# A delta rule's instructions put in order per engine by a list scheduler inside the kernel, with one projection ahead of them and one behind

## The chip, the core and the metric

The kernel runs on one core of a Trainium2 chip. The metric is the time of one execution on the device in microseconds, as the median of three runs. Engines: PE (tensor engine, its weight loads shown apart as PEld), DVE (vector), ACT (scalar), POOL (GpSimd), SP (issues the weight transfers).

## The reference

Two blocks run one after the other in fp32. The first has two layers over 256 context and 256 latent tokens; its even layer mixes a windowed attention with a delta rule ("rwkv7"). The stage in question is this recurrence, run forward and backward, first over the context, then over the latent tokens, for 8 heads of 64:

```
def rwkv7_scan(f, d, s0, reverse):
    def step(state, inp):
        r_t, w_t, k_t, v_t, kk_t, a_t = inp
        sa = jnp.einsum('bhvk,bhk->bhv', state, -kk_t)
        state = (state * w_t[:, :, None, :] + sa[..., None] * (kk_t * a_t)[:, :, None, :]
                 + v_t[..., None] * k_t[:, :, None, :])
        return state, jnp.einsum('bhvk,bhk->bhv', state, r_t)
    ...
    s_last, ys = lax.scan(step, s0, xs, reverse=reverse)
```

Its inputs come from a shifted projection of the tokens, its output is normalised per head, gated, joined with the attention's and multiplied by `w_out`. The feed-forward parts, the odd layer and the second block follow; the change leaves them alone.

## The kernel before

The scan is written as blocks of 64 tokens. There are sixteen passes n, in the order of three loops (L1062 to L1066): tile t (two heads) from 0 to 3, sequence s (context, latent), direction d. A pass is two functions.

`rwkv_par` (L819) needs no state. Preparation: the decays (`pw` L832, `sg`, a scan `cs`, three exponentials), the rates (`pa` L850, `ic`), the scaled vectors `kr` and `bk`, their products `gp` (L883) with masked copies into `GK` and `Gt`, and transposes (`pbk`, `pkv`). Inverse: a product `px`, then five doubling levels (L931 to L944), each a DVE transposition `Tp`, eight matmuls `pq`, a masked DVE copy `Qm` and eight matmuls `psx`; then `pwu`, `pqm` and `QM`. `rwkv_rec` (L973) takes the state through four blocks: matmul `yp` (L986), a copy by DVE and one by ACT (L993), the next matmul; then it copies to `yN`.

Passes overlap as far as buffers allow. PSUM banks go by rings (L180): the preparation takes banks 0, 1, 2 in turn, the inverse of pass n bank 3 + n % 3, the recurrence bank 6, everything else of the stage bank 7 (`B_A`). `kr`, `Gt`, `GA`, `KX` and `QM`, `RHS` and `lam` have four slots (n % 4), `GK`, `bk`, `sg`, `cs`, `ic`, `b_` two.

Between the passes stand `kappa(t)` (L788), `gates_out` and `rwkv_out` (L1006, L1018: normalise, transpose `pyt`, gate, split into `moA`), and twelve `ada_chunk`s (L315), the modulation for later stages: each loads four blocks of 512 KB (`wada`) into the three slots `raw` that all weights share, and multiplies them (L331). Before the third pass `proj_a((3, 7, 11), B_LATE)` (L1068) projects the last tile's r, k and v (`psT`, L259 to L261, then `evac_a`). Before the last `rwkv_rec`, `proj0` (L1074) multiplies the attention's half `moB` by `w_out` (`pso`, L264 to L266) for token tiles 0 and 1; after the last `rwkv_out` the `moA` half follows (L1090), and then tiles 2 and 3.

What sets the order now: the framework's scheduler takes the instructions by priority, which is the order of the program, places each on its engine when its own timing model has it ready, and hands out buffers as they come free. Each engine then works its queue strictly in that order.

## Time and profile before

| | us |
|---|---|
| median of 3 runs (1882.54 to 1882.95) | 1882.9 |
| the profiled execution | 1893.0 |
| its span, first to last instruction | 1891.2 |
| preparation of the first pass to the last `pyt` | about 188 to 612 |

The page gives for each engine its busy time, its share of the span and the number of its instructions; busy times of PE overlap with each other's modelled ends, so that for small matmuls the number of instructions in a stretch says more. The views by stretch give the same per stretch, with the granted PE clock (1.00 is 2.4 GHz, 0.50 is 1.2 GHz, between them a mean). Lines are those of the kernel before.

### The profile page before, as it was taken

The page shows a single profiled execution, that of the slowest core. Times are in us where ns is not written, and L with a number is a line of the kernel's source. Part 1 is how long each engine was busy: PE and PEld are TensorE (multiplying, and loading weights), DVE is VectorE, ACT ScalarE, POOL GpSimd, SP SyncE. Part 2 cuts the span into 40 slices and gives each one's busy share as a digit, 9 for nine tenths or more (in the row PEclk, how much of TensorE's full clock was granted, in tenths as well). Part 3 has the DMA queues.
Part 4 walks back from the last instruction along what each step waited for, and adds up shares of the span by engine and source line. Part 5 has one row for each costly group of instructions (what it writes and reads, how often), then busy time and mean ns, then how long its engine had stood idle before and what let it go on. Part 6 is the DMA issues. An engine that isn't in the chain of part 4 may idle for free.

```text
span 1891.2 us, 33833 instructions
## 1 busy us (share of the span) xinstructions
PE 1785.9 (94%) x13505; PEld 1479.0 (78%) x13505; DVE 1081.5 (57%) x1973; ACT 884.7 (47%) x1707; POOL 451.4 (24%) x528
## 2 busy tenths in 40 slices
PE   6999899999887999999999999899998999999998
PEld 4777577566765787888887886699987879989997
DVE  3676566555653632444447674545556787558676
ACT  4554344333333545433335554445545545446554
POOL 2120434334410334433333303211111122110000
PEclk9999899998888899999999999989999999999999
DMA  9321420213125525544432321246655634555653
GB/s 308 101 57 45 123 91 2 90 46 97 40 69 169 186 81 159 163 138 139 134 123 78 90 88 56 89 126 194 193 167 179 201 101 133 180 178 165 192 179 123
DMA packets 185405, 240.06 MB, mean 127 GB/s; under 512 B 8960, under 2 KB 127888, under 8 KB 185120
## 3 DMA queue, kind: packets, MB, share of 16 engines
q1 hardware_dynamic: 183056, 229.68, 39.0%
q0 software_dynamic: 1904, 7.70, 1.2%
q8 instruction: 106, 1.74, 0.4%
q14 instruction: 51, 0.42, 0.1%
q10 hardware_dynamic: 288, 0.52, 0.1%
HBM read 236.83 MB, written 1.05 MB: 126 GB/s over the span
## 4 chain that ended last, share of the span: by engine, by line
PE 55%; DMA 3%; DVE 3%; ACT 2%; issue 2%; POOL 1%; SPq 0%; POOLq 0%; DVEq 0%; ACTq 0%
PE psT L259 7%; PE psT L260 7%; PE psT L261 7%; PE pf L264 5%; PE pf L265 5%; PE pf L266 5%; PE psU L259 2%; PE psU L261 2%; PE psU L260 2%; DMA wadc<-in_w_ada_dram 2%; PE psN L435 1%; PE psO L723 1%; PE psS L677 1%; PE psP L713 1%; PE psX L264 1%
## 5 line engine op out<-in xcount | busy, mean ns | idle before, releaser
L245 DVE TENSOR_TENSOR wlo<-raw,whi 128x1024 fp32r<-128x1024 f32 x328 | 403.3, 1236 | 283.1 <-ACT whi L244 279.3
L244 ACT ACTIVATE whi<-raw 128x1024 fp32r<-128x1024 f32 x328 | 345.6, 1056 | 286.0 <-PE psT L260 136.5
L259 PE MATMUL psT<-uh,whi 128*128 128x256 f32 (+1 forms) x1184 | 384.3, 329 | 2.7 <-ACT uh L545 0.8
L260 PE MATMUL psT<-ul,whi 128*128 128x256 f32 (+1 forms) x1184 | 382.8, 324 | 0.2 <-DVE ul L302 0.2
L261 PE MATMUL psT<-uh,wlo 128*128 128x256 f32 (+1 forms) x1184 | 379.9, 324 | 0.0
L259 PEld LDWEIGHTS psT<-uh,whi 128*128 128x128 f32 x1184 | 224.0, 191 | 25.2 <-issue 2.2
L260 PEld LDWEIGHTS psT<-ul,whi 128*128 128x128 f32 x1184 | 224.3, 190 | 22.1 <-issue 2.4
L261 PEld LDWEIGHTS psT<-uh,wlo 128*128 128x128 f32 x1184 | 224.3, 190 | 18.9 <-issue 0.7
L265 PE MATMUL pf<-wlo,hh 128*128 128x512 f32 x472 | 182.4, 390 | 1.1 <-DVE wlo L245 1.1
L266 PE MATMUL pf<-whi,hlo 128*128 128x512 f32 x472 | 182.4, 390 | 0.0
L264 PE MATMUL pf<-whi,hh 128*128 128x512 f32 x472 | 182.0, 392 | 0.0
L1131 POOL TENSOR_TENSOR ffr<-ffr 128x512 f32<-128x512 f32 (+1 forms) x64 | 66.2, 1035 | 284.2 <-ACT hh L1130 252.7
L265 PEld LDWEIGHTS pf<-wlo,hh 128*128 128x128 f32 x472 | 88.6, 188 | 19.0 <-DVE wlo L245 1.4
L266 PEld LDWEIGHTS pf<-whi,hlo 128*128 128x128 f32 x472 | 88.6, 188 | 18.8 <-issue 0.2
L264 PEld LDWEIGHTS pf<-whi,hh 128*128 128x128 f32 x472 | 88.5, 188 | 17.5
L259 PE MATMUL psU<-uh,whi 128*128 128x256 f32 x352 | 99.2, 283 | 1.0 <-DVE cv L1704 1.0
L260 PE MATMUL psU<-ul,whi 128*128 128x256 f32 x352 | 98.7, 281 | 0.0
L261 PE MATMUL psU<-uh,wlo 128*128 128x256 f32 x352 | 98.6, 280 | 0.0
L1132 DVE TENSOR_TENSOR hlo<-ffr,hh 128x512 fp32r<-128x512 f32 (+1 forms) x64 | 46.5, 727 | 79.0 <-POOL ffr L1131 79.0
L353 POOL TENSOR_TENSOR adac<-adac,wadc 128x512 f32<-128x512 f32 x56 | 75.0, 1340 | 68.1 <-ACT wadc L351 54.3
L351 ACT ACTIVATE wadc<-wadc,sT 128x512 f32<-128x512 f32 x56 | 40.5, 723 | 102.4 <-DMA wadc<-in_w_ada_dram 102.3
L259 PEld LDWEIGHTS psU<-uh,whi 128*128 128x128 f32 x352 | 66.6, 190 | 1.9 <-ACT whi L244 0.9
(680 smaller groups left out, 3358.1 us busy)
## 6 DMA issues: line engine op xcount, KB each, us to landing
raw<-in_w_ff_dram SPq DMA_DIRECT2D x128, 512.0 KB, 4.5
wada<-in_w_ada_dram SPq DMA_DIRECT2D x64, 512.0 KB, 4.5
raw<-in_w_in_dram SPq DMA_DIRECT2D x50, 512.0 KB, 4.3
raw<-in_w_ffn_up_dram SPq DMA_DIRECT2D x44, 512.0 KB, 4.6
wadc<-in_w_ada_dram SPq DMA_DIRECT2D x64, 256.0 KB, 2.9
raw<-in_w_out_dram SPq DMA_DIRECT2D x24, 512.0 KB, 4.1
raw<-in_w_ffn_down_dram SPq DMA_DIRECT2D x22, 512.0 KB, 4.5
raw<-in_w_in_even_dram SPq DMA_DIRECT2D x21, 512.0 KB, 5.1
```

The source lines that it names most:

```text
L244: S.activation(hi[:, :tot], raw[:, :tot], AF.Copy)
L245: V.tensor_tensor(lo[:, :tot], raw[:, :tot], R(hi[:, :tot]), op=OP.subtract)
L259: T.matmul(p_, wh, xh, start=first, stop=False)
L260: T.matmul(p_, wh, xl, start=False, stop=False)
L261: T.matmul(p_, wl, xh, start=False, stop=last)
L264: T.matmul(p_, xh, wh, start=first, stop=False)
L265: T.matmul(p_, xh, wl, start=False, stop=False)
L266: T.matmul(p_, xl, wh, start=False, stop=last)
L351: S.activation(d_, w, AF.Copy, scale=sT[:, k, 0:1])
L353: G.tensor_tensor(acc, acc, w, op=OP.add)
L1131: G.tensor_tensor(r_, r_, r_, op=OP.mult)
L1132: V.tensor_tensor(hl_, r_, R(hh), op=OP.subtract)
```

## The change

A class `_Flow` records the stage's instructions and gives them out in an order of its own. While it is on, an engine call is put on a list with what it reads and writes, a length by a formula per engine, and a time until others see its end; consecutive matmuls into one tile form one entry. `links` finds the dependences, and for each entry the longest chain `way` that hangs on it. `order` is a list scheduler: among the entries that can start within 150 ns of the earliest, the one with the longest `way` is next on its engine. `close` gives the instructions to the framework with the order fixed on PE, DVE, ACT and POOL; SP's order, and where instructions from outside fall between them, stays the scheduler's. `_Ring` gives each tile of a tag a fixed place, n modulo the number of buffers, in the program's order; `_Heir` lets `moA` take the place of tiles that are then dead. All passes, `kappa`, `gates_out`, `rwkv_out` and the chunks are on the list. `proj_a((3, 7, 11))` comes ahead of it, and both calls of `proj0` for tiles 0 and 1 behind it.

```diff
+class _Ring:
+    def __init__(self, flow, pool, bufs):
+        self.flow, self.pool, self.bufs, self.places = flow, pool, bufs, {}
+    def tile(self, shape, dtype, name, tag=None, bufs=None):
+        kw = {k: v for k, v in (("tag", tag), ("bufs", bufs)) if v is not None}
+        if not self.flow.on:
+            return self.pool.tile(shape, dtype, name=name, **kw)
+        n, slots = self.places.setdefault(tag or name, [0, []])
+        self.places[tag or name][0] += 1
+        i = n % (bufs or self.bufs)
+        if i == len(slots):
+            slots.append(self.pool.tile(shape, dtype, name=name, **kw))
+        t_ = slots[i]
+        if list(t_.shape) == list(shape):
+            return t_
...
+class _Engine:
+    def __init__(self, flow, eng, key):
+        self.flow, self.eng, self.key = flow, eng, key
+    def __getattr__(self, op):
+        f = getattr(self.eng, op)
+        if not self.flow.on:
+            return f
+        return lambda *a, **k: self.flow.take(self.key, op, f, a, k)
+class _Heir:
+    def __init__(self, old, make):
+        self.old, self.make, self.new = old, make, None
+    def __getitem__(self, k):
+        return _Part(self, lambda t_: t_[k])
+    def get(self):
+        if self.new is None:
+            self.new = self.make()
+        return self.new
+class _Part:
+    def __init__(self, heir, view):
+        self.heir, self.view = heir, view
+        self.old = view(heir.old)
+    def bitcast(self, dt):
+        return _Part(self.heir, lambda t_: self.view(t_) if t_ is self.heir.old else self.view(t_).bitcast(dt))
+    def get(self):
+        return self.view(self.heir.get())
+class _Flow:
+    def __init__(self, tc):
+        self.tc, self.on, self.ops = tc, False, []
+    def eng(self, eng, key):
+        return _Engine(self, eng, key)
+    def pool(self, pool, bufs=1):
+        return _Ring(self, pool, bufs)
...
+    def take(self, key, op, f, a, k):
...
+        o.tail = 70
+        if key == "T":
+            mv, st = (a[1], a[1]) if op == "transpose" else (a[2], a[1])
+            n = math.prod(mv.shape[1:]) if op != "transpose" else a[2].shape[1]
+            rows, cols = st.shape[0], st.shape[1]
+            share = (1 if rows > 64 or cols > 64 else .5) if cols > 32 else .25
+            if rows <= 64 < cols:
+                share = .5
+            cyc = 2 if op == "transpose" else 4 if mv.dtype == F32 else 1
+            o.dur, o.mode, o.tail = n * cyc * share / 2.4 + 6, (rows > 64, cols > 64, cols > 32), 270
+        elif key == "V":
+            o.dur = (150 + 1.03 * n * (2 if op.endswith("scan") else 1)) if psum or n < 200 else 170 + 1.2 * n
+        elif key == "S":
+            o.dur = 200 + .83 * n
+        elif key == "G":
+            o.dur = 1650 if k.get("op") == OP.pow else 150 + 2.3 * n
+        else:
+            o.dur, o.tail = 2800, 2500
+        p = self.ops[-1] if self.ops else None
+        if key == "T" and p is not None and p.key == "T" and p.w[0][0] == o.w[0][0] and p.mode == o.mode:
+            p.calls += o.calls
+            p.res += o.res
+            p.w += o.w
+            p.r += o.r
+            p.dur += o.dur
+        else:
+            self.ops.append(o)
...
+    def links(self):
+        seen = {}
+        for i, o in enumerate(self.ops):
+            o.pre = set()
+            mine = [(x, True) for x in o.w] + [(x, False) for x in o.r]
+            for (nm, q, m, ps), wr in mine:
+                for j, q2, m2, wr2 in seen.get(nm, ()):
+                    if q & q2 and ((wr or wr2) and m & m2 or ps and self.ops[j].key != o.key):
+                        o.pre.add(j)
+            for (nm, q, m, ps), wr in mine:
+                l = seen.setdefault(nm, [])
+                if wr:
+                    l[:] = [e for e in l if e[0] == i or e[1] & ~q or e[2] & ~m or (ps and self.ops[e[0]].key != o.key
+                            and False)]
+                l.append((i, q, m, wr))
+        for i in range(len(self.ops) - 1, -1, -1):
+            o = self.ops[i]
+            o.way = getattr(o, "way", 0) + o.dur
+            for j in o.pre:
+                p = self.ops[j]
+                p.way = max(getattr(p, "way", 0), o.way + p.tail)
+    def order(self, slack=150, sem=70):
+        self.links()
+        ops = self.ops
...
+            best = None
+            for i, t in ready.items():
+                o = ops[i]
+                st = max(t, free.get(o.key, 0))
+                if best is None or st < best:
+                    best = st
+            cand = [i for i, t in ready.items() if max(t, free.get(ops[i].key, 0)) <= best + slack]
+            i = max(cand, key=lambda i: (self.prio(ops[i]), -i))
+            o = ops[i]
+            st = max(ready.pop(i), free.get(o.key, 0))
+            d = o.dur
+            if o.key == "T":
+                if mode != o.mode:
+                    d += 100
+                mode = o.mode
+            free[o.key] = st + d
+            out.append((st, i))
+            for j in nxt[i]:
+                left[j] -= 1
+                ops[j].at = max(getattr(ops[j], "at", 0), st + d + (o.tail if ops[j].key != o.key else 0))
+                if not left[j]:
+                    ready[j] = ops[j].at
+        return [i for _, i in sorted(out)]
+    prio = staticmethod(lambda o: o.way)
+    def close(self, engines):
+        self.on = False
+        seq = self.order()
+        with self.tc.manual_schedule(engines=engines):
+            for i in seq:
+                o = self.ops[i]
+                for (f, a, k), r in zip(o.calls, o.res):
+                    b = f(*[x.get() if isinstance(x, _Part) else x for x in a], **k)
+                    r.ins = getattr(b, "ins", None)
+        self.ops = []
...
 @with_exitstack
 def body(ctx: ExitStack, tc: tile.TileContext, A, out, dbg=None):
     nc = tc.nc
-    V, S, G, T = nc.vector, nc.scalar, nc.gpsimd, nc.tensor
+    flow = _Flow(tc)
+    V, S, G, T, Q = (flow.eng(*x) for x in ((nc.vector, "V"), (nc.scalar, "S"), (nc.gpsimd, "G"), (nc.tensor, "T"),
+                                            (nc.sync, "Q")))
     R = lambda ap: ap.bitcast(F32)
 
     LAT, CTX = 0, 1
     cp = ctx.enter_context(tc.tile_pool(name="cp", bufs=1))
-    sm = ctx.enter_context(tc.tile_pool(name="sm", bufs=4))
-    psp = ctx.enter_context(tc.tile_pool(name="psp", bufs=1, space=PSUM))
+    sm = flow.pool(ctx.enter_context(tc.tile_pool(name="sm", bufs=4)), 4)
+    psp = flow.pool(ctx.enter_context(tc.tile_pool(name="psp", bufs=1, space=PSUM)))
 
     def ring(*banks):
 
@@ -216,7 +432,7 @@
     def wraw(W, r0, kt, c0, n, name="raw"):
         t_ = hl[0].tile([128, 1024], F32, name=name, tag="raw", bufs=hl[1])
         v_ = t_[:, :kt * n].rearrange("p (k c) -> p k c", k=kt)
-        nc.sync.dma_start(v_, W[r0:r0 + kt * 128, c0:c0 + n].rearrange("(k p) c -> p k c", p=128))
+        Q.dma_start(v_, W[r0:r0 + kt * 128, c0:c0 + n].rearrange("(k p) c -> p k c", p=128))
         return t_, v_
 
     mark = {}
@@ -322,7 +538,7 @@
                     _, w = wraw(A["w_ada"][l], q * 256, 2, j * 512, 512, name="wada")
                 else:
                     w = pool.tile([128, 1024], F32, name="wada", tag="wada", bufs=6).rearrange("p (k c) -> p k c", k=2)
-                    nc.sync.dma_start(w, A["w_ada"][l][q * 256:q * 256 + 256, j * 512:j * 512 + 512]
+                    Q.dma_start(w, A["w_ada"][l][q * 256:q * 256 + 256, j * 512:j * 512 + 512]
                                 .rearrange("(k p) c -> p k c", p=128))
                 ws += [w[:, 0, :], w[:, 1, :]]
 
@@ -452,7 +668,7 @@
     def opool(name, bufs=1, side=None):
         cm = tc.tile_pool(name=name, bufs=bufs, side=side)
         opened.append(cm)
-        return cm, cm.__enter__()
+        return cm, flow.pool(cm.__enter__(), bufs)
 
     def cpool(*cms):
         for cm in cms:
@@ -1040,8 +1256,9 @@
         G.tensor_tensor(o_[:, tk], o_[:, tk], bvt[t][:, tk], op=OP.add)
         if not moA[t]:
 
-            moA[t] = [mix.tile([128, 512], F32R, name=f"moA{a}{t}", tag=tag, bufs=4)
-                      for a, tag in zip("hl", ("rT", "kT") if t < 3 else ("vT", "vT"))]
+            moA[t] = [_Heir(rkv[j], lambda a=a, tag="rkv"[j // 4] + "T": mix.tile(
+                [128, 512], F32R, name=f"moA{a}{t}", tag=tag, bufs=4))
+                for a, j in zip("hl", (t, 4 + t) if t < 3 else (8, 9))]
         split(moA[t][0][:, tk], moA[t][1][:, tk], o_[:, tk])
 
     moA = [None] * 4
@@ -1059,19 +1276,16 @@
     ps0 = {}
     later = [(0, j) for j in range(4, 12)] + [(1, j) for j in range(4)]
     n = 0
+    proj_a((3, 7, 11), B_LATE)
+    cpool(cm_u)
+    cm_rb, rb[0] = opool("rwb", side="left")
+    flow.on = True
     for t in range(4):
         if t == 0:
             kappa(0)
         for s in range(2):
             for d in range(2):
-                if n == 2:
-                    proj_a((3, 7, 11), B_LATE)
-                    cpool(cm_u)
-                    cm_rb, rb[0] = opool("rwb", side="left")
                 st = rwkv_par(n, t, d, s)
-                if n == 15:
-                    ps0 = {(i, ch): B_O0("pso") for i in range(2) for ch in range(2)}
-                    proj0((0, 1), (0, 1), (2, 3))
                 rwkv_rec(n, t, d, s, st)
                 n += 1
                 for a in later[len(later) * (n - 1) // 16:len(later) * n // 16]:
@@ -1086,7 +1300,10 @@
                 if t < 3 and n % 4 == 3:
                     kappa(t + 1)
     rwkv_out(3, (1,))
-
+    flow.close({x.engine for x in (nc.tensor, nc.vector, nc.scalar, nc.gpsimd)})
+    moA[:] = [[x.get() for x in m] for m in moA]
+    ps0 = {(i, ch): B_O0("pso") for i in range(2) for ch in range(2)}
+    proj0((0, 1), (0, 1), (2, 3))
     proj0((0, 1), (0, 1), (0, 1))
     cpool(cm_rb, cm_rw, cm_rc)
     if dbg == "mix0":
```

## Rows read from the trace of the kernel before

**Rows 1.** The page: its head, and busy us, share and instructions by engine.

```profile
span 1891.2 us, 33833 instructions
...
PE 1785.9 (94%) x13505; PEld 1479.0 (78%) x13505; DVE 1081.5 (57%) x1973; ACT 884.7 (47%) x1707; POOL 451.4 (24%) x528
```

**Rows 2.** By stage: length, busy PE, PEld, DVE, ACT, POOL (instructions), clock, DMA.

```profile
224.00:612.00 388.00, 343.98 (x4770) 252.47 (x4768) 215.07 (x547) 150.92 (x404) 128.48 (x193) 0.91 0.25 79
```

**Rows 3.** The same stage for `pso` alone, then for L331 alone (PE first).

```profile
224.00:612.00 388.00, 32.69 (x115) 22.85 (x116) 0.00 (x0) 1.38 (x4) 0.91 0.25 79
...
224.00:612.00 388.00, 34.35 (x171) 4.62 (x168) 0.91 0.25 79
```

**Rows 4.** Three finer stretches, columns as in rows 2.

```profile
250.00:300.00 50.00, 48.26 (x842) 37.32 (x838) 34.47 (x93) 22.81 (x68) 21.53 (x34) 1.00 0.14 45
...
350.00:400.00 50.00, 44.02 (x523) 27.19 (x524) 23.08 (x64) 17.32 (x50) 16.92 (x27) 0.90 0.24 75
...
480.00:500.00 20.00, 18.39 (x399) 15.73 (x397) 13.13 (x34) 9.63 (x28) 8.25 (x14) 1.00 0.01 3
```

**Rows 5.** Timeline: start us, length us, engine, line, operation, tiles, count.

```profile
264.77 0.49 PE L986 MATMUL yp<-S,QM 128*128 128x128 f32 x2
...
265.19 0.68 PE L939 MATMUL pq<-Tp,GA 64*64 64x64 f32 x16
...
265.95 0.42 DVE L941 TENSOR_TENSOR Qm<-pq,cst_c 128x256 f32<-128x256 f32 x1
...
266.38 0.45 DVE L933 STREAM_TRANSPOSE Tp<-psx 128x256 f32<-128x256 f32 x1
...
266.95 0.39 PE L986 MATMUL yp<-S,QM 128*128 128x128 f32 x2
...
271.26 0.47 ACT L834 ACTIVATE sg<-pw,hw 128x256 f32<-128x256 f32 x1
...
273.42 0.39 ACT L924 ACTIVATE KX<-px 128x256 f32<-128x256 f32 x1
...
277.52 1.06 PE L331 MATMUL psA<-wada,sT 128*32 128x512 f32 x8 [0.25 <-DMA wada<-in_w_ada_dram]
...
277.99 0.42 DVE L864 TENSOR_TENSOR bk<-ic,cs 128x256 f32<-128x256 f32 x1
...
306.49 0.37 ACT L946 ACTIVATE Sp<-psx 128x256 f32<-128x256 f32 x1
```

**Rows 6.** Waits in 224 to 612 us: waited in total, times, longest.

```profile
PE psA L331 <- DMA wada<-in_w_ada_dram: 16.7, 10, 3.4
```

**Rows 7.** Timeline of ACT: start of passes three and seven, end of three.

```profile
232.07 0.47 ACT L834 ACTIVATE sg<-pw,hw 128x256 f32<-128x256 f32 x1
...
304.10 0.47 ACT L834 ACTIVATE sg<-pw,hw 128x256 f32<-128x256 f32 x1
304.45 0.76 ACT L1002 ACTIVATE yN<-yp 64x256 f32<-64x256 f32 x2
```

**Rows 8.** `psT` alone, by stage; then the timeline around the first level.

```profile
188.00:224.00 36.00, 19.57 (x72) 14.44 (x72) 5.08 (x7) 2.44 (x4) 0.86 0.35 103
...
214.14 0.45 DVE L933 STREAM_TRANSPOSE Tp<-Sp 128x256 f32<-128x256 f32 x1 [2.14 <-POOL Sp L929]
...
219.66 0.39 PE L261 MATMUL psT<-uh,wlo 128*128 128x512 f32 x1
...
221.06 0.40 PE L261 MATMUL psT<-uh,wlo 128*128 128x512 f32 x1
...
223.96 0.68 PE L939 MATMUL pq<-Tp,GA 64*64 64x64 f32 x16
```

**Rows 9.** Timeline of the stage's end.

```profile
586.50 0.83 POOL L967 TENSOR_TENSOR QM<-QM,lam 128x384 f32<-128x384 f32 x1 [27.42 <-DVE QM L963]
...
605.24 1.22 PE L264 MATMUL pso<-whi,moBh 128*128 128x512 f32 x2 [5.22 <-ACT whi L244]
...
610.64 0.38 PE L1037 MATMUL pyt<-cst_ci,yN 128*128 128x128 f32 x2
```

More of the change, by code (lines that the diff above doesn't have):

```diff
@@ L149 @@
 _NPV = _pvn
+class _Ring:
[13 more added lines that the diff above has]
+            return t_
+        dims = " ".join("abcdefg"[:len(t_.shape) - 1])
+        v_ = t_.rearrange(f"p {dims} -> p ({dims})") if len(t_.shape) > 2 else t_[:, :]
+        v_ = v_[:shape[0], :math.prod(shape[1:])]
+        if len(shape) == 2:
+            return v_
+        d = "abcdefg"[:len(shape) - 1]
+        return v_.rearrange(f"p ({' '.join(d)}) -> p {' '.join(d)}", **dict(zip(d[1:], shape[2:])))
@@ new lines, with touched @@
+class _Part:
[6 more added lines that the diff above has]
+        return self.view(self.heir.get())
+class _Op:
+    ins = None
+class _Flow:
[5 more added lines that the diff above has]
+        return _Ring(self, pool, bufs)
+    @staticmethod
+    def touched(x):
+        if isinstance(x, _Part):
+            x = x.old
+        if isinstance(x, tile.Tile):
+            x = x[tuple(slice(None) for _ in x.shape)]
+        t_ = x.tensor
+        free = math.prod(t_.shape[1:])
+        (_, np_), *dims = x.ap
+        p0, o = divmod(x.offset, free)
+        idx = np.zeros(1, np.int64) + o
+        for st, n in dims:
+            idx = (idx[:, None] + st * np.arange(n)).ravel() if st else idx
+        m = 0
+        for i in np.unique(idx).tolist():
+            m |= 1 << i
+        return t_.name, sum(1 << q for q in range(p0 // 32, (p0 + np_ + 31) // 32)), m, t_.space == PSUM
+    def take(self, key, op, f, a, k):
+        is_ap = lambda x: isinstance(x, (tile.Tile, bass.AP, _Part)) and not (
+            isinstance(x, bass.AP) and not isinstance(x.tensor, tile.Tile))
+        aps = [x for x in list(a) + list(k.values()) if is_ap(x)]
+        outs = [x for x in (a[0], k.get("accum_out")) if x is not None and is_ap(x)]
+        o = _Op()
+        o.key, o.calls, o.res = key, [(f, a, k)], [o]
+        o.w = [self.touched(x) for x in outs]
+        o.r = [self.touched(x) for x in aps if not any(x is y for y in outs)] + (o.w if key == "Q" else [])
+        first = next(x for x in aps)
+        n = math.prod((first.old if isinstance(first, _Part) else first).shape[1:])
+        psum = any(t_[3] for t_ in o.w + o.r)
+        o.tail = 70
[25 more added lines that the diff above has]
+            self.ops.append(o)
+        return o
+    def links(self):
[22 more added lines that the diff above has]
+        ops = self.ops
+        nxt, left = [[] for _ in ops], [len(o.pre) for o in ops]
+        for i, o in enumerate(ops):
+            for j in o.pre:
+                nxt[j].append(i)
+        ready, free, mode = {i: 0 for i, n in enumerate(left) if not n}, {}, None
+        out = []
+        while ready:
+            best = None
[20 more added lines that the diff above has]
+                    ready[j] = ops[j].at
+        self.span = max(free.values())
+        return [i for _, i in sorted(out)]
[10 more added lines that the diff above has]
+        self.ops = []
```

## The prediction, made before the changed kernel was built

> **What bounds the kernel now.** I read the page first, then the busy time by stage, then finer stretches, then the timeline inside one of them, and last the waits. The page [rows 1] gives the profiled execution a span of 1891.2 us and shows PE (the tensor engine) busy for 94% of it, DVE for 57%; the whole execution took 1893.0 us, where the median of the three timed runs is 1882.9 us. So the sums below are made against 1893.0 and the difference is carried to 1882.9.
>
> The stage that the change touches is the delta rule: sixteen passes (4 tiles t, two sequences s, two directions d), each one `rwkv_par` and one `rwkv_rec`. The first correction of the doubling levels starts at 223.96 us [rows 8], the transposes of the last output tile stand at 610.64 us [rows 9]; I call 224 to 612 us the stage. PE is shown busy 343.98 of its 388 us [rows 2]. That looks like a full engine, and it is not one: ends of small matmuls are modelled and overlap. What counts is how many PE instructions pass in a microsecond. The stage holds 4770 PE instructions [rows 2]. Of these 115 are 512-column matmuls of the output projection (`pso`) and 171 are those of the modulation chunks (L331) [rows 3]; the other 4484 are small ones of the delta rule. The projection's matmuls follow each other by 0.232 us where nothing holds them (as the same shape does in `psT`: six steps from 219.66 to 221.06 us, of which [rows 8] has the first and the last, are 0.233 us each), so 115 of them are 26.7 us. Eight L331 take 1.06 us [rows 5], so 171 are 22.7 us. That leaves 388 - 26.7 - 22.7 = 338.6 us for 4484 small instructions: **75.5 ns each**.
>
> The same trace shows what they cost when PE is fed [rows 4]: 842 instructions in 250 to 300 us are 59.4 ns each, 399 in 480 to 500 us are 50.1 ns each, both at a granted clock of 1.00, that is 2.4 GHz throughout. In 350 to 400 us it is 523, or 95.6 ns, and the clock is 0.90, so for a fifth of the time it was at 1.2 GHz. So the same work runs at two very different paces inside one stage, with the same buffers, and PE is the engine that the best stretches fill; DVE with 215.07 us, ACT with 150.92 us and POOL with 128.48 us [rows 2] are well below it.
>
> Why the pace drops is in the timeline [rows 5]. A level is one group of 16 PE instructions (0.68 us), a masked copy on DVE (0.42 us), a second such group, and a DVE transposition (0.45 us): 2.23 us, and with four hand-overs of 0.08 us (265.19 + 0.68 to 265.95) some 2.6 us. Five levels are 13 us. The fourth pass has its KX copy just before the levels at 273.42 us and the copy just after them at 306.49 us: 33.1 us. About 20 us of that is waiting behind other passes' instructions on in-order queues. A pass keeps its buffers that long: the third one starts at 232.07 us and its last result is copied at 304.45 us, 72 us later, and the pass that takes the same one of four slots starts at 304.10 us [rows 7]. Four passes in 72 us are 18 us a pass; the stage as a whole needs 388/16 = 24 us. The waits [rows 6] also show PE standing 16.7 us for the modulation weights, with the delta rule's instructions behind them in the queue.
>
> **The change part by part.**
> *The order.* No instruction is added to or taken from the delta rule, the chunks, `kappa`, `gates_out` and `rwkv_out`; the counts above stay. What changes is the sequence on PE, DVE, ACT and POOL, chosen by the length of the chain that still hangs on each instruction, where now the scheduler goes by program order among what it thinks ready. The slots and PSUM banks keep their number. A pass that waits for nothing I estimate at some 40 us: from its `sg` to its `bk` 271.26 to 278.41, that is 7 us [rows 5]; 4 us more, by the lengths of its instructions, to the first level; 13 us of levels; 5 us to `QM`; and for the recurrence four steps of 2.2 us (264.77 to 266.95 [rows 5]) and 2 us around them. Four slots would then allow one pass in some 10 us, so order and not slots should set the pace, and PE's own load should be next. I bound the new pace by the best and by the present one: 50.1 ns (20 us held it) and 75.5 ns. I take 59.4 ns, the pace that lasted 50 us, and no better, since the list's durations are fixed numbers and chunks, `kappa` and `rwkv_out` must be fitted in. 4484 x 59.4 = 266 us, at 50.1 ns 225 us, at 75.5 ns 339 us.
>
> *The chunks.* They stay 171 x 1.06/8 = 22.7 us of PE. The list gives each weight transfer a fixed slot of time, so I cost their waits at nothing: the cover is the other passes' work placed ahead of them. If a transfer is late, everything behind it on PE waits; uncovered that is at most today's 16.7 us [rows 6] again.
>
> *The end.* In the last pass nothing is left to overlap with: the last `QM` is scaled at 586.50 us and the stage ends 25 us later [rows 9], with recurrence, sums, a POOL power and transposes one after another. At the pace above I have counted only some 60 of its instructions (3 us), so I add 22 us.
>
> *Projection all ahead* (`proj_a` for 3, 7 and 11). Its 72 matmuls [rows 8] are 72 x 0.233 = 16.8 us. They now lie between 188 and 221.46 us, while the first two passes are being prepared, and hold up the first level: its transposition starts at 214.14 and ends at 214.59 us, the group that needs it starts at 223.96 us, 9.4 us late. Ahead of the delta rule they follow the earlier projection directly (its last group ends near 187.5 us) and would end near 204.5 us. The first level needs about 25 us from the first `pw` to that transposition. With all of it after the projection the level starts at 229 us, with the preparation woven in at 215 us. I take 224 us: nothing won or lost, plus 5 or minus 9. Its three weight transfers of 512 KB pass SP before the chunks', whose transfers come later by that; these have slack.
>
> *Output projection behind* (`proj0` for `moB`, and its loads). Today 115 of the 192 `pso` matmuls are done before 612 us, in holes that the last passes leave. Written after the region, they may still be put into its last stretch, once banks 0, 1, 2 and 4 come free, that is after the preparation of the last pass; the 22 us above are such holes, against 26.7 us of matmuls. I count 8 us that show up after the end (between 0 and 26.7 us). In the trace of before, the second load of the weights already held PE 5.22 us there [rows 9].
>
> **The sum.** 224 + 266 + 23 + 22 = 535 us for the end of the stage, against 612: 77 us won; less 8 us behind it: 69 us. 1893.0 - 69 = 1824 us for a profiled execution, and 1882.9 - 69 = **1814 us**.
>
> **The rivals.**
> *Slots bind, the moves cost (slower).* If what ends a pass's wait is a free slot or bank and not its place in the queue, the pace stays at 75.5 ns. For it: pass seven starts within 0.4 us of the end of pass three [rows 7]; places are now handed out strictly in program order, and a ring of three banks has to carry six or seven tiles of each preparation. Against it: 59.4 and 50.1 ns were reached with the same slots [rows 4], and a pass spends 20 of 33 us of its levels waiting. Then the moves are bare cost: 5 us at the start and about 15 of the 26.7 us behind: 1882.9 + 20 = 1903 us. It decides from 74.8 ns on, where 224 + 4484 x 74.8 ns + 23 + 22 + 8 is 612. I give it 13%. The Trainium skill has a rule on its side (Perfetto Trace Analysis, Optimization Strategy): the same gap again and again on the engine that ought to be full can mean that there is no SBUF or PSUM for the next tile. By that rule an order without more buffers wins nothing, and the time would be this rival's. The trace agrees that slots are handed on at once, but not that they are the cause.
>
> *Half way.* The list's plan is upset by what it doesn't model: DVE copies stretched beside POOL, late transfers, halved clock. Then the pace is between 67.5 and 74.8 ns, 36 to 69 us worse than the sum: 1850 to 1883 us, most of it still faster. 12%.
>
> *Denser than any 50 us of before.* 50.1 ns or less throughout: 42 us better, 1772 us or less. 5%.
>
> *No real change.* The new order runs like the old one and the moves cancel: within 0.2%. That is the upper edge of the half-way case and 3% of it.
>
> **How the numbers follow.** Forecast with a pace of 52 to 67.5 ns: 70%. The range takes the fast end at 50.1 ns (1772) with 4 us off for a start at 215 us in part, 1768 us, and at the slow end 67.5 ns (1850) with 5 us for the start and 11 more us behind the end, 1866 us. Faster by over 0.2% (3.8 us, about what a measurement of this kernel can tell from no change): 70 + 5 + 9 = 84%; within 0.2%: 3%; slower: 13%.
>
> **What would show it.** After the change the stage should hold about as many PE instructions in 310 us, its 50-us stretches near 840 instead of 520 to 840, the levels of a pass should take 20 to 25 us instead of 33, a pass should hold its slot some 60 us, DVE should be near 70% busy in the stage, and the granted clock nearer to 1.00 than to the 0.91 of now [rows 2]. The projections `psT` of L566's last three tiles should end before the first `pq`. Wrong would be: a pace still over 70 ns; passes that still start the moment that a slot comes free, with PE idle; PE waiting in front of L331 for longer than now; or the won time standing again as a block of `pso` matmuls and loads between the last `pyt` and the first matmul of the feed-forward part.

## The result, and the profile after

The changed kernel takes 1857.3 us (median of four executions, 1851.8 to 1859.6) against 1882.9 us: a ratio of 0.9858, 95% interval 0.9834 to 0.9882, or 25.6 us less. The forecast was 1814 us, so 43 us of the expected gain are missing. The page of after, as [rows 1]:

```profile
span 1849.8 us, 33850 instructions
...
PE 1759.9 (95%) x13505; PEld 1471.3 (80%) x13505; DVE 1092.5 (59%) x1973; ACT 885.4 (48%) x1707; POOL 457.2 (25%) x528
```

The whole profiled execution took 1851.8 us, the fastest of the four. From profile to profile the span is 41.4 us shorter, from median to median the time is 25.6 us. The difference is in the two samples: the profiled execution of before (1893.0 us) lies above all 59 executions of before that were timed beside the experiments (1875.0 to 1889.8 us).

All instructions of the list carry line 361 now, and tiles go by the name that their place was given first: `px` for the tiles of the inverse, `psr` and `ssp` for those of the preparation, `KX` for `QM`, `psA` for bank 7. By stage, columns as in [rows 2]: the whole, the part up to 520 us, the rest.

```profile
224.00:575.00 351.00, 324.74 (x4799) 248.07 (x4796) 227.06 (x550) 153.70 (x408) 140.23 (x198) 0.96 0.28 90
224.00:520.00 296.00, 279.37 (x4534) 213.85 (x4532) 203.95 (x513) 133.25 (x376) 135.36 (x192) 0.97 0.24 76
520.00:575.00 55.00, 45.37 (x269) 34.23 (x269) 23.11 (x37) 20.44 (x33) 4.86 (x7) 0.91 0.52 166
```

The same stretches for `pso` alone (the whole, then up to 520 us) and for the chunks' matmuls out of `wada` alone (the same two), PE first:

```profile
224.00:575.00 351.00, 35.98 (x131) 25.45 (x132) 0.00 (x0) 1.36 (x4) 0.96 0.28 90
...
224.00:520.00 296.00, 0.00 (x0) 0.00 (x0) 0.00 (x0) 0.00 (x0) 0.97 0.24 76
...
224.00:575.00 351.00, 24.69 (x180) 3.52 (x176) 0.96 0.28 90
224.00:520.00 296.00, 22.56 (x164) 3.17 (x160) 0.97 0.24 76
```

So the stage has two parts. Up to 520 us it holds 4534 - 164 = 4370 small instructions in 296 - 164 x 1.06/8 = 274.3 us, which is 62.8 ns each (75.5 in before, 59.4 forecast; over the whole stage, reckoned as the 75.5 were, it is 66.1). The last 55 us hold only 122 of them, with 131 matmuls of the output projection. The stage ends with the last `pyt` at 573.3 us, where before it was 610.6 us.

The waits of PE from 215 to 575 us, the two that matter here (waited in total, times, longest); of the first, before had one wait of 5.22 us [rows 9], and the second was 16.7 us there [rows 6]:

```profile
PE pso L480 <- ACT whi L460: 8.2, 3, 4.4
...
PE psA L361 <- DMA wada<-in_w_ada_dram: 1.8, 2, 1.0
```

Where passes start, from the timeline of ACT: passes 13 and 14, counted from 0 (the `sg` out of a PSUM bank).

```profile
434.63 0.48 ACT L361 ACTIVATE sg<-ssp,hw 128x256 f32<-128x256 f32 x1
...
473.54 0.46 ACT L361 ACTIVATE sg<-psr,hw 128x256 f32<-128x256 f32 x1
```

And from that of DVE, the last results of passes 11 and 13:

```profile
469.75 0.84 DVE L361 TENSOR_TENSOR yN<-yN,yp 64x256 f32<-64x256 f32 x2 [0.99 <-PE yp L361]
...
495.44 0.84 DVE L361 TENSOR_TENSOR yN<-yN,yp 64x256 f32<-64x256 f32 x2
```

Pass 14 starts only when passes 12 and 13 alone are left, 39 us after pass 13, though the slot of pass 14 had been free since the end of pass 10 at 457.8 us. The list takes what has the longest chain behind it, and the last two passes have the shortest. Its own reckoning (`self.span` of `order`, 305 us in all) has the same gap, from 205 to 242 us after its start: the first product of pass 14 could start at 218 us there and is taken at 242, so this is planned and not an accident. Passes 4 and 8 start after such gaps too (248.3 to 284.1 and 327.8 to 354.2 us). From 496 us to the end two passes are alone on the chip.

### The profile page after: what moved, and what is told of

Same layout as the page of the kernel before. It is cut to its first block, busy times and chain, and to the rows that moved or that the text cites. A ratio compares the mean times of both kernels' runs of the same rounds, so it can differ in the third digit from the quotient of the medians.

```text
span 1849.8 us, 33850 instructions
## 1 busy us (share of the span) xinstructions
PE 1759.9 (95%) x13505; PEld 1471.3 (80%) x13505; DVE 1092.5 (59%) x1973; ACT 885.4 (48%) x1707; POOL 457.2 (25%) x528
## 4 chain that ended last, share of the span: by engine, by line
PE 59%; DVE 3%; issue 2%; DMA 1%; ACT 1%; POOL 1%; SPq 0%; POOLq 0%; DVEq 0%; ACTq 0%
PE psT L475 8%; PE psT L477 8%; PE psT L476 8%; PE pf L480 6%; PE pf L481 6%; PE pf L482 6%; PE psU L475 2%; PE psU L477 2%; PE psU L476 2%; PE psN L651 1%; PE psO L939 1%; PE psS L893 1%; PE psP L929 1%; DVE wlo L461 1%; PE psX L480 1%
```

## Experiments

Each ran beside the kernel before on the same chip; the ratio is to that, with its 95% interval. "Played through" in the expectations means: the sequence of the list followed in order with durations read from the trace of after. Differences between two runs are those of their medians. The runs stand on several chips, where the medians of before go from 1880.1 to 1884.8 us; reckoned from the ratios, such a difference comes out up to 4 us otherwise.

### Which part of the change gives the gain

`moves_alone`: the kernel before, with only the two moves.

```diff
+    proj_a((3, 7, 11), B_LATE)
+    cpool(cm_u)
+    cm_rb, rb[0] = opool("rwb", side="left")
...
+    ps0 = {(i, ch): B_O0("pso") for i in range(2) for ch in range(2)}
+    proj0((0, 1), (0, 1), (2, 3))
```

> The kernel before with the two moves of the change and nothing else: the projection of tiles 3, 7 and 11 ahead of the delta rule, the output projection's first half written behind it. No list, no fixed places. Theory 'the order gave less than forecast, the moves are nearly free' (what the trace of after says: first level at 224.5 us, 36 us between the last transposes of the output and the first feed-forward matmul in both kernels): 1883 to 1891 us, so the list by itself is worth 26 to 34 us. Rival 'the moves took the gain back': 1898 to 1910 us, so the list by itself would be worth 41 to 53 us. Should it be under 1878 us, the moves and not the list carry part of the 25.6 us.

1886.9 us, 1.0027 (1.0010 to 1.0044): 3 to 5 us slower.

`places_only`:

```diff
-        seq = self.order()
-        with self.tc.manual_schedule(engines=engines):
+        seq = range(len(self.ops))
+        if True:
```

> The changed kernel with its fixed places and both moves, but its delta-rule instructions are handed over in program order and nothing holds the engines to an order, so the framework's scheduler sorts them. Theory 'the held order is what gains': 1885 to 1905 us, that is the moves alone or worse by what the fixed places cost (each tile's place is now chosen in program order). Rival 'fixed places by themselves free the passes': 1857 us or less.

1886.5 us, 1.0006 (0.9981 to 1.0030).

`list_no_hold`:

```diff
-        with self.tc.manual_schedule(engines=engines):
+        if True:
```

> The changed kernel with the list's sequence handed over as the program order, but nothing holds the engines to it. If the sequence is what counts and the scheduler keeps near it: 1850 to 1865 us, like the changed kernel. If holding the engines to it is what counts: 1880 to 1905 us, like program order. If holding to a sequence made from fixed durations is itself a cost (an engine waits for its next instruction in the list though a later one could run): under 1850 us.

1890.6 us, 1.0037 (1.0019 to 1.0055). The same stretch as above holds 4043 PE instructions there, 4534 in after:

```profile
224.00:520.00 296.00, 274.70 (x4043) 201.20 (x4042) 173.91 (x456) 120.31 (x342) 119.84 (x181) 0.93 0.20 66
```

So neither moves, nor places, nor the sequence handed over as a proposal gain anything. The gain comes only when the engines are held to the list's sequence, and the moves alone cost 3 to 5 us. A kernel held to the order of the program was not run, so what holding does without the list is not shown.

### Do slots bind?

`three_slots` and `before_three_slots`:

```diff
-    NY, NZ = 4, 3
+    NY, NZ = 3, 3
```

> The changed kernel with three slots for the passes in place of four (NY 4 to 3), the list made anew. Theory 'order and engine load set the pace, slots do not': within 8 us of the changed kernel, 1849 to 1865 us; the list's own reckoning with its fixed durations ends at 303 us, with four slots at 305 us. Rival 'slots bind': a pass holds a slot for some 66 us (its first sg to its yN in the trace of after), three slots then allow one pass in 22 us and 16 passes need 352 us and more, and waits for slots appear at every pass: 1880 us or more.

> The kernel before with three slots for the passes in place of four (NY 4 to 3), nothing else. Theory 'a pass waits for its turn in the queues, not for a slot': within 8 us of the kernel before, 1875 to 1891 us. Rival 'slots bind in the kernel before' (pass seven starts as pass three ends): a pass holds its slot some 72 us, three slots allow one pass in 24 us with no room left, 16 passes then take 384 us and the start and end come on top: 1900 to 1930 us.

The changed kernel: 1845.2 us, 0.9787 (0.9770 to 0.9804). The kernel before: 1881.8 us, 1.0007 (0.9988 to 1.0026). A slot fewer costs nothing in either. With three slots in the kernel before, the seventh pass takes the slot of the fourth, whose last result is copied at 322 us, and starts all the same where it did (304.10 us in [rows 7]):

```profile
304.60 0.47 ACT L834 ACTIVATE sg<-pw,hw 128x256 f32<-128x256 f32 x1
```

So that it starts there as a slot comes free was coincidence. Why three slots are 12 us faster in the changed kernel isn't settled; with the other edits below the same step gave 4 us.

### Is TensorE full?

```diff
+                for g in (2, 3, 0, 1) * (2 if flow.on and h == 0 else 0):
+                    T.matmul(p_[32 * g:32 * g + 32, :], sT[:, 4 * h + g, :], ws[g], start=True, stop=True)
```

> The changed kernel with the matmuls of the twelve modulation chunks issued twice (the first half's three times, the extra ones overwritten), the list made anew: 192 more TensorE instructions, 192 x 1.06/8 us = 25.4 us of TensorE, nothing else. Theory 'TensorE is full for most of the stage after the change, so the forecast's 266 us for the delta rule was near the floor of the engine and only the holes at the batch borders and the tail were left out': the list cannot hide it all, 12 to 25 us more than the changed kernel, 1869 to 1882 us (the list's own reckoning ends at 328 us, 23 more than without). Rival 'the stage waits on latency and has TensorE time to spare': 1855 to 1866 us.

1865.7 us, 0.9909 (0.9884 to 0.9933): 8 us more for 25.4 us of work. My theory expected 12 us or more, so it fell: two thirds of the added work found room. The number isn't clean, since the clock at the start was higher with the extra matmuls too (granted 0.80 in 210 to 220 us, 0.50 in after).

### The output projection in the list's way

`pso_held`: its weights are split only after the last pass's `Wt`.

```diff
+        self.last = [o.ins for o in self.ops if o.key == "S" and o.w[0][0].startswith("Tp")][-1]
...
+    behind[:], free[0] = [flow.last], 0
     proj0((0, 1), (0, 1), (2, 3))
     proj0((0, 1), (0, 1), (0, 1))
+    behind[:] = []
```

> The changed kernel, but the splitting of the output projection's weights on ACT and DVE may start only after the last pass's Wt copy, so none of its matmuls can stand among the delta rule before the last pass's levels are done. In the trace of after 93 of its 192 matmuls stand there before 562 us (93 x 0.233 is 21.7 us of TensorE), ACT stands 15.9 us for its weights and TensorE 6.7 us for the split. Theory 'they lie in the list's way': the stage ends 15 to 25 us earlier, and of the 21.7 us some 10 find room beside the last recurrence: 1840 to 1855 us. Rival 'they only fill holes': the stage ends where it did and the matmuls come behind it: 1865 to 1880 us.

1844.8 us, 0.9811 (0.9770 to 0.9851): 12.6 us better by the medians, 9 by the ratios, with intervals that overlap; the same edit on top of the bonus, below, is clear of that. The trace of after shows what stood in the way. First, from the last pass's last level to the scaling of its `QM`:

```profile
518.69 0.45 DVE L361 STREAM_TRANSPOSE Tp<-px 128x256 f32<-128x256 f32 x1 [1.13 <-PE px L361]
...
522.77 0.68 PE L361 MATMUL px<-Sp,Qm 64*64 64x64 f32 x16
...
526.79 1.06 ACT L460 ACTIVATE whi<-raw 128x1024 fp32r<-128x1024 f32 x1 [6.68 <-DMA raw<-in_w_out_dram]
...
528.10 0.38 ACT L361 ACTIVATE Sp<-px 128x256 f32<-128x256 f32 x1
...
541.74 0.83 POOL L361 TENSOR_TENSOR KX<-KX,lam 128x384 f32<-128x384 f32 x1 [21.16 <-DVE KX L361]
```

The level's second product is computed at 523.5 us; its copy `Sp` stands behind a split for which ACT waits 6.68 us. From the transposition to the scaling it is 23.1 us, in `pso_held` 13.2:

```profile
527.17 0.45 DVE L361 STREAM_TRANSPOSE Tp<-px 128x256 f32<-128x256 f32 x1 [1.14 <-PE px L361]
...
540.32 0.83 POOL L361 TENSOR_TENSOR KX<-KX,lam 128x384 f32<-128x384 f32 x1 [11.27 <-DVE KX L361]
```

From there to the last `pyt` it is 31.6 us in after and 28.2 in `pso_held` (568.5 us). So the two stretches together are 13 us shorter. That the two profiled executions differ by 5 us only lies ahead of them: the last level comes 8.5 us later in `pso_held`, whose clock is 0.51 in 230 to 240 us where after has 1.00. Second, one step of the last pass's recurrence in after:

```profile
543.86 0.38 PE L361 MATMUL yp<-S,KX 128*128 128x128 f32 x2
545.36 1.06 ACT L460 ACTIVATE whi<-raw 128x1024 fp32r<-128x1024 f32 x1 [5.44 <-DMA raw<-in_w_out_dram]
546.32 0.58 ACT L361 ACTIVATE adar<-psA 128x512 f32<-128x512 f32 x1
546.45 1.23 DVE L461 TENSOR_TENSOR wlo<-raw,whi 128x1024 fp32r<-128x1024 f32 x1 [4.88 <-ACT whi L460]
...
547.07 1.06 ACT L460 ACTIVATE whi<-raw 128x1024 fp32r<-128x1024 f32 x1 [0.17 <-DMA raw<-in_w_out_dram]
547.71 0.23 DVE L361 COPY S<-yp 64x64 f32<-64x64 f32 x1
...
548.16 0.21 ACT L361 COPY S<-yp 64x64 f32<-64x64 f32 x1
...
550.13 0.62 PE L480 MATMUL pso<-whi,moAh 128*128 128x512 f32 x2
...
550.58 0.38 PE L361 MATMUL yp<-S,KX 128*128 128x128 f32 x2
```

The step is computed at 544.2 us, but its two copies stand behind a split for which ACT waits 5.44 us for a transfer, and DVE 4.88 us for ACT. They are done at 548.4 us; the other 2.2 us go to `pso` matmuls that stand ahead in PE's own queue. The next step starts at 550.6, 6.7 us after this one. With the splitting held, waits in 520 to 575 us shrink from the first pair of rows (after) to the second (held):

```profile
DVE wlo L461 <- ACT whi L460: 24.6, 9, 4.9
ACT whi L460 <- DMA raw<-in_w_out_dram: 23.0, 8, 6.7
```

```profile
DVE wlo L462 <- ACT whi L461: 12.2, 9, 3.4
ACT whi L461 <- DMA raw<-in_w_out_dram: 10.5, 6, 4.5
```

### What makes the sequence good

`meas_stay` has two edits, `list_measured` and `list_stay` one each.

```diff
+    def measured(o):
...
+        tab = {("T", "px", 8): 515, ("T", "px", 4): 490, ("T", "yp", 16): 1000, ("T", "psA", 4): 930,
+               ("V", "bk", 1): 684, ("V", "cs", 1): 866, ("V", "ic", 1): 740, ("V", "b", 1): 565,
+               ("G", "KX", 1): 876, ("G", "kr", 1): 851, ("G", "lam", 1): 313, ("G", "sqy", 1): 1323}
...
-            i = max(cand, key=lambda i: (self.prio(ops[i]), -i))
+            i = max(cand, key=lambda i: (self.prio(ops[i]) + 2000 * (getattr(ops[i], "mode", 0) == mode), -i))
```

> The changed kernel with the list's fixed durations replaced by those measured in the trace of after (a group of eight 64x64 products 515 ns, the scan 866, a product on DVE out of SBUF 684, kr on POOL 851, reductions 570; from TensorE to another engine 220 ns, between others 50), and with a bonus of 2 us in the choice for a TensorE group of the same operand shape as the last one (in the trace of after such a group follows in 0.515 us, one of another shape in 0.61). Played through with the measured durations, after's sequence ends at 329 us and this one at 313. Theory 'the sequence is worse than it need be, since the list reckons with wrong durations': 1837 to 1848 us. Rival 'the sequence is not what limits, what is not in the list does (output projection, late weights, clock)': 1852 to 1862 us.

1840.6 us, 0.9795 (0.9767 to 0.9823), as the theory of the durations had it. But the two edits had not been told apart:

> The changed kernel with the measured durations in the list and nothing else (four slots, no bonus for the same operand shape). Played through with the measured durations its sequence ends at 317 us, after's at 329, durations and bonus together at 313. Theory 'wrong durations made the sequence worse': 1842 to 1850 us, most of the 17 us that both together gave. Rival 'the changes of operand shape did': 1853 to 1860 us.

1847.6 us, 0.9824 (0.9793 to 0.9855).

> The changed kernel with the bonus for a TensorE group of the same operand shape and nothing else (durations as in the change). Played through with the measured durations its sequence ends at 324 us, after's at 329. Theory 'wrong durations made the sequence worse': 1850 to 1858 us, at most 6 us of gain. Rival 'the changes of operand shape did': 1840 to 1847 us.

1832.7 us, 0.9741 (0.9714 to 0.9767): the other way round. The bonus alone, one line, gives 24.6 us, as much as the whole change had given; the durations alone give 9.7, and added to the bonus they take some of it back.

> The changed kernel with the list's window of choice at 100 ns in place of 150 and nothing else: a perturbation of the sequence with no aim. The list's own reckoning ends at 304.6 us (305.2 before), played through with the measured durations at 330 (329). If sequences that reckon alike run alike: within 4 us of the changed kernel, 1853 to 1861 us. If the time of a sequence is largely a matter of chance: 8 us or more away in either direction, and single steps of that size in the other runs prove little.

`other_slack`: 1850.2 us (1848.1 to 1864.9), 0.9835 (0.9788 to 0.9883): 7 us from the changed kernel, with intervals that overlap. I read it as the size that a perturbation of the sequence can have by itself. The bonus is well outside it. Holding the output projection is too, where it is measured on top of the bonus (below: 10.6 us, with intervals apart); the durations alone hardly, and three slots alone hardly either.

How the bonus does it, in the stage of `list_stay` (up to 495 us, which has 152 chunk matmuls and no `pso`, and the rest):

```profile
225.00:495.00 270.00, 254.93 (x4425) 199.34 (x4426) 195.77 (x506) 129.86 (x369) 134.87 (x190) 1.00 0.25 80
495.00:550.00 55.00, 48.52 (x373) 36.82 (x370) 24.76 (x44) 23.21 (x40) 6.51 (x7) 0.97 0.55 183
```

(270 - 152 x 1.06/8)/(4425 - 152) is 58.5 ns an instruction, 4.3 ns under after: 4370 x 4.3 ns are 19 of the 27 us by which its stage ends earlier (last `pyt` 546.2 us). In the trace of after, groups whose operands were ready early follow each other like this (timeline of PE):

```profile
428.42 0.68 PE L361 MATMUL px<-Sp,Qm 64*64 64x64 f32 x16
429.03 1.16 PE L361 MATMUL ssp<-kr,bk 64*128 64x128 f32 x8
...
436.19 0.68 PE L361 MATMUL px<-Sp,Qm 64*64 64x64 f32 x16
436.70 1.10 PE L361 MATMUL px<-Tp,GA 64*64 64x64 f32 x32
```

After sixteen 64x64 instructions the next group starts 0.51 us later where its operands have the same shape and 0.61 us later where not (medians of 62 and 52 such steps: 0.515 and 0.612). After one product `kr`,`bk` it is 0.224 and 0.313 us (medians of 96 and 24 steps). So a change costs about 0.10 us, which is what the list reckons for one, but only after it has chosen. By its own count the bonus takes the changes from 322 to 263: at 0.10 us each that is 6 of the 19 us. The clock is a second difference: it is 0.97 in the 296 us of after and 1.00 here, which by 0.03 x 296 is up to 9 us, and whether the denser sequence kept it up or had it by chance is not shown. The rest is open. The Trainium skill (TensorEngine Tiling (Array Packing), Tiling Modes, Key Properties) says that changing the tiling mode drains TensorE. The steps above agree; the page gives no price.

### Putting the edits together

> The changed kernel with the bonus for the same operand shape and the output projection held back until the last pass's levels; four slots, durations as in the change. If the 12 us that holding gave on the changed kernel add to the bonus's 24: 1818 to 1826 us. If the bonus already had that gain (its stage ended 25 us earlier): 1828 to 1838 us.

`stay_held`: 1822.1 us, 0.9666 (0.9650 to 0.9682): the two add up, with two short edits.

> As the run with measured durations and the bonus for the same operand shape, with three slots in place of four. Played through with the measured durations its sequence ends at 310 us (329 for the changed kernel, 325 for the changed kernel with three slots, which ran 12 us faster than four). If both add up: 1822 to 1836 us. If three slots gain only by another sequence, which the new durations replace: 1837 to 1848 us. If a sequence fitted to durations has no room for four-slot overlap left and three slots then bind: over 1848 us.

`meas_stay_3`: 1836.2 us, 0.9772 (0.9746 to 0.9799).

> Measured durations, the bonus for the same operand shape, three slots, and the output projection held back until the last pass's levels, together. If the gain of holding it (12 us on the changed kernel) adds to the other three (21 us): 1822 to 1830 us. If the faster sequence already keeps the output projection in holes (138 of its matmuls stood before 560 us in the run without holding, against 86 in the changed kernel): 1834 to 1845 us.

`meas_stay_held_3`: 1831.2 us, 0.9712 (0.9688 to 0.9735), between the two theories.

`proj_in_list`: beside measured durations, bonus and held output projection,

```diff
-    NY, NZ = 4, 3
+    NY, NZ = 2, 3
...
-    proj_a((3, 7, 11), B_LATE)
-    cpool(cm_u)
-    cm_rb, rb[0] = opool("rwb", side="left")
     flow.on = True
+    proj_a((3, 7, 11), B_LATE)
```

Two smaller edits go with it: an entry of the list takes no further matmul once it is 1750 ns long, which splits the projection's groups alone, and the pools are opened and closed to fit.

> As the run before (measured durations, bonus, output projection held back), with the projection of tiles 3, 7 and 11 put into the list in place of ahead of it, and two slots in place of three (its operands keep the room of the others). In the trace of after the stage's first 20 us, 205 to 225, have nearly only the first passes' preparation: TensorE's granted clock there is 0.91, 0.50 and 0.74 of full speed in three stretches of 10 us, and in other runs of the same start it stays at 0.50 to 245 us. Theory 'the projection ahead cost its 17 us and the clock': by the list the 17 us go into these holes and the clock stays up, 8 to 15 us less than without, 1812 to 1826 us. Rival 'two slots bind' or 'the projection delays the first levels as it did before the change': 1835 us or more.

1819.1 us, 0.9658 (0.9638 to 0.9678), with two slots.

> The best kernel so far (1819 us) with the projection of tiles 3, 7 and 11 put back ahead of the list; measured durations, bonus, held output projection and two slots stay. Theory 'the projection ahead costs its time and the clock of the first levels': 1829 to 1838 us, as with three slots (1831 us). Rival 'the last step came from two slots': 1817 to 1823 us. If two slots bind when the projection is ahead: over 1840 us.

`two_slots_ahead`: 1828.4 us, 0.9718 (0.9690 to 0.9745): of the 12 us from three slots with the projection ahead to the best kernel, 9 are the projection's place. How much of that is the clock and how much the matmuls put into holes isn't told apart. Ahead of it first, in the list second (10 us each from 200 us; the last three numbers are clock, DMA share and GB/s):

```profile
200.00:210.00 10.00, 9.01 (x39) 4.76 (x37) 4.72 (x9) 2.60 (x6) 2.91 (x5) 0.91 0.01 2
210.00:220.00 10.00, 7.20 (x30) 5.20 (x27) 3.63 (x8) 1.46 (x4) 3.84 (x7) 0.50 0.32 106
220.00:230.00 10.00, 8.07 (x76) 4.86 (x75) 5.79 (x12) 3.69 (x10) 6.60 (x10) 0.74 0.34 105
```

```profile
200.00:210.00 10.00, 10.00 (x68) 7.67 (x67) 6.24 (x13) 4.16 (x9) 4.04 (x6) 1.00 0.28 85
210.00:220.00 10.00, 10.00 (x107) 8.02 (x106) 6.95 (x16) 3.09 (x9) 6.47 (x10) 1.00 0.06 22
220.00:230.00 10.00, 10.00 (x181) 7.73 (x180) 4.68 (x11) 4.88 (x13) 3.55 (x7) 1.00 0.01 3
```

The first is the changed kernel: the projection is done at 204 us, TensorE has 30 instructions in 210 to 220 us, and the granted clock is 0.50, that is 1.2 GHz.

> The best kernel so far (1819 us) with the list's durations as in the change in place of the measured ones; bonus, held output projection, projection in the list and two slots stay. Played through with the measured durations its sequence ends at 337 us, the best kernel's at 317. Theory 'durations matter': 1830 to 1840 us. Rival 'the other edits carried it': 1815 to 1823 us.

`stay_proj_in_list`: 1830.2 us, 0.9712 (0.9692 to 0.9731): in this kernel the durations are worth 11 us, though with four slots and the bonus they were worth -8. The sign depends on the rest, so what better durations are worth stays open.

## Why the prediction was wrong, step by step

The direction was right and the range (1768 to 1866 us) holds the result. The forecast of 1814 us is 43 us too low. Of these, 10 come from the base, 28 from the sum, and 5 from after's profile being that much under its median.

**The base.** I made the sum against the profiled execution and carried the whole difference to the median. The 10 us by which that execution was slow were treated as something that the change leaves alone. The 59 other executions say that they were a matter of that one sample. The safer sum starts at the median and takes absolute times with care.

**The order: right in kind, 3.4 ns too good.** 62.8 ns against 59.4 over 4370 instructions are 15 us. The 59.4 were themselves a little off: 16 of the 842 instructions [rows 4] are chunks' matmuls, and without them it is 58.0 ns for the small ones alone. The measured pace is inside the forecast's own 52 to 67.5 ns, and the rival of the slots (74.8 ns) and the half-way case (67.5 ns) are both off. My reason for not taking it lower was that the list's durations are fixed numbers; what the runs improved was the choice itself. With changes of operand shape made rarer, which I had not looked at, the pace was 58.5 ns, a little below the forecast; the price of a change explains a third of that gain, and the rest is open.

**The end: the step that failed.** I took 22 us from the scaling of the last `QM` to the last `pyt` and let the forecast's pace hold for all that lies ahead of it. In fact 122 small instructions lie in the last 55 us; 122 at 59.4 ns, two us of chunks and the 22 would be 31, so 24 us are missing here. Some 10 of them lie behind the scaling (31.6 us in place of 22), the others ahead of it. 13 are shown: by so much `pso_held` is shorter from the last level to the last `pyt`, so they are the output projection in the queues, above all its splits, for which ACT and DVE stood. For the other 11 I have an account and no run. I had taken the end of the kernel before as a guide [rows 9], where the last passes overlapped with what came ahead of them, and did not ask in which order a rule of the longest remaining chain takes the last two passes: last, together, and with nothing beside them. No run lets these passes start earlier and changes nothing else.

**Output projection behind: wrong sign, and in the wrong place.** I counted 8 us behind the stage and nothing inside it. Behind it nothing was lost: from the last `pyt` to the first feed-forward matmul it is 38 us in both kernels (573.3 to 611.2, and 610.6 to 648.4). Inside, 131 of its matmuls were pulled into the tail. I had named the holes that would hide them and the 5.22 us that PE stood for a split [rows 9], but not that ACT and DVE would stand too, with the copies of the last level and of the recurrence queued behind. That is the gain of `pso_held`, half of what the end lacks.

With 15 + 24 us the stage ends at 574 in place of 535 us; the 8 us behind did not come, and 4 us were won elsewhere: 39 - 8 - 4 = 27, against 69 - 41.4 = 27.6.

**Chunks.** Right: 180 matmuls in the stage, and PE waited 1.8 us for weights in place of 16.7.

**Projection ahead.** The first level's products start at 224.5 us (224 forecast). What I left out is the clock: I had PE idle there at no cost. Against the projection in the list, its place ahead cost 9 us, clock and matmuls together.

**Signs named beforehand.** The stage in 310 us: 351. Stretches near 840 in 50 us: by 20 us between 240 and 520 they run from 192 to 400, so the dips stayed. The levels of a pass in 20 to 25 us: 25 to 36 from the first `KX` copy to the last `Sp` copy. Slots held for some 60 us: 58 to 80. DVE near 70%: 227.06 of 351 is 65%. Clock nearer 1.00: 0.96.

**The rivals.** Slots do not bind, and the rule of consistent bubbles that I gave 13% (the Trainium skill, Perfetto Trace Analysis, Optimization Strategy) does not describe this stage: with a slot fewer the time was the same before the change and lower after it. With the bonus and the projection held, 1822 us is reached by the mechanism of the forecast, so its size was within reach of the idea and not of this list.

## What to carry to other kernels

A sequence that the engines are held to loses where something outside it gets between: an instruction of the next stage that waited for a transfer stopped the queue of every engine it sat in, so put it into the list or hold it back. Look at the end of a list made by longest remaining chain first: here the last two passes, with the shortest chains, were taken last and ended up alone. And before reading much into one reordering, run one that is only perturbed: here that alone moved the median by 7 us, though with intervals that overlap.

## What the runs showed of the hardware

A change of operand shape on TensorE cost 0.10 us after a group of sixteen 64x64 instructions (0.612 against 0.515 us) and 0.09 us after a single 64x128 product (0.313 against 0.224 us). With the projection done at 204 us and only the preparation left for TensorE, the granted clock was 0.50 in 210 to 220 us. It was back at 1.00 from 230 us in the changed kernel, but still at 0.50 in 230 to 240 us in `meas_stay_held_3`; why it rose earlier in the one stays open. 25.4 us of added TensorE work cost 8 us. An instruction that waits for a transfer holds up what stands behind it on its engine: ACT stood 6.68 us for a weight with the copy `Sp` behind it.
